# Decoder trunk on one core: elementwise sums move from GpSimd to VectorE, TensorE and adding transfers

## The chip, the core and the metric

The kernel runs on one NeuronCore of a Trainium2 chip. The engines are called as in the profile: PE (TensorE, matrix products), DVE (VectorE), ACT (ScalarE), POOL (GpSimd), SP (SyncE, which here only starts transfers). Transfers are started from a queue of an engine and carried out by 16 DMA engines. The metric is the time of one execution on the device in microseconds (us).

## The reference, cut to what matters

All numbers are fp32; T = 528 tokens (16 of them learned), D = 1024 channels. Two layers, each a mixer and a gated MLP:

```
h = h + fox_conformer_mixer(rms_norm(h))         # layer 0
   proj = x @ w_in                               # q, k, v, f (8 heads of 64), glu (2 x 512)
   a, g = split(glu);  u = a * sigmoid(g)
   u = causal_depthwise_conv(u, conv_w) + conv_b # width 31, 512 channels
   u = silu(layer_norm(u))
   out = concat(forgetting_attention(q, k, v, f), u) @ w_out
h = h + conv_glu_ffn(rms_norm(h))                # up to 2 x 2816, conv of width 3, silu(gate)*val, down
h = h + multiscale_pool_mixer(rms_norm(h))       # layer 1: windows 2, 4, 8, 16 over the tokens
   d_g = (cs - lag_w(cs)) / min(n, w) - x        # cs = cumsum over tokens, g = channel group
   y   = (d @ pool_w[g] + pool_b) * pool_scale
h = h + conv_glu_ffn(rms_norm(h))
out = rms_norm(h)[:, 16:]
```

## The kernel before, in words

Channels lie on the 128 partitions and tokens along them, so h is 8 tiles h0 to h7 of 128x528; what is 528 wide is multiplied in two halves of 264. PE works in the reduced fp32 format: every operand is split in a high part (a rounding copy) and a low part (the rest), and each product is three matmuls, wH with xH, wH with xL, wL with xH.

**Weights.** They come in 162 chunks of 8 tiles (512 KB), in the order in which PE wants them, through 3 buffers (4 in the second half). `prepare(c)` makes each chunk: SP's queue loads `raw`, ACT (or DVE for the 20 chunks in `VECTOR_CHUNKS`) copies it to `wH`, ACT writes `wL` = -wH, and POOL's queue starts a transfer that adds `raw` onto `wL` (L179, `accum_op=add`). This adding transfer is the only one of its size before the change.

**Stages of the trace.** Start and first norm to 34 us; the mixer of layer 0 to 286 us; its MLP ("up" and "dn" products) to 666 us; the pooling mixer, with the first up tiles of the second MLP inside it, to 722 us; the rest of that MLP and the output to the end.

**The mixer.** `PE_ORDER` sets PE's order by hand: pairs of a/g projections, then q, k, v by head pairs, with the attention's products between them. The convolution has 4 tiles of 31 taps each. Tap 0 is on ACT. A tap of kind 0 is one DVE instruction (L495: cv += u shifted, times its column of weights); one of kind 1 is a product on ACT into `tap` (2 buffers, L498) and an addition on POOL (L499). Tiles 0 and 2 and 28 taps of tile 3 are kind 0 (88 instructions), tile 1 and taps 1 and 2 of tile 3 kind 1 (32). `fill(pace)`, called at each F of `PE_ORDER`, hands out taps of both kinds by the table `PACE`. DVE also empties PE's sums (u L465, sg L472, q L561, k L579, v L598, o L738), splits the attention's weights (PL L718) and takes its row maxima (L660). `ln_sum` adds up the four convolved tiles for the layer norm (`mu`), on POOL.

**The pooling mixer.** PE's and DVE's orders are written out by `POOL_ORDER`: Z scales z (the normalised h) by the norm's R, S is the window sum (for windows over 2 a scan), T the ratio at the first 16 tokens, D makes the difference and adds it to h (L1037), X splits h in xH (ACT) and xL (DVE, L260) and multiplies it with four up tiles, Q squares h for the next norm (ACT) and adds the square to `acc` (POOL, L249).

## Time and profile before

| | us |
|---|---|
| median of 3 runs | 1096.94 (1095.26 to 1097.67) |
| the profiled execution | 1095.61 |
| its span in the profile | 1093.5 |
| PE busy | 1037.5 (95%) |
| DVE busy | 586.6 (54%) |
| ACT busy | 622.4 (57%) |
| POOL busy | 306.1 (28%) |

The span runs from the first instruction to the last; the profiled execution's own time has some 2 us around it. The shares of busy time are means over stages that differ: PE is full in both MLPs and has its idle time at the start, in the mixer to 165 us, and in the pooling mixer.

### The profile page before, as it was taken

The page shows a single profiled execution, that of the slowest core. Times are in us where ns is not written, and L with a number is a line of the kernel's source. Part 1 is how long each engine was busy: PE and PEld are TensorE (multiplying, and loading weights), DVE is VectorE, ACT ScalarE, POOL GpSimd, SP SyncE. Part 2 cuts the span into 40 slices and gives each one's busy share as a digit, 9 for nine tenths or more (in the row PEclk, how much of TensorE's full clock was granted, in tenths as well). Part 3 has the DMA queues.
Part 4 walks back from the last instruction along what each step waited for, and adds up shares of the span by engine and source line. Part 5 has one row for each costly group of instructions (what it writes and reads, how often), then busy time and mean ns, then how long its engine had stood idle before and what let it go on. Part 6 is the DMA issues. An engine that isn't in the chain of part 4 may idle for free.

```text
span 1093.5 us, 20138 instructions
## 1 busy us (share of the span) xinstructions
PE 1037.5 (95%) x8356; PEld 1023.8 (94%) x8356; DVE 586.6 (54%) x868; ACT 622.4 (57%) x872; POOL 306.1 (28%) x397
## 2 busy tenths in 40 slices
PE   7988789999999999999999998789999999999996
PEld 6978689999999999999999998789999999999995
DVE  5799999886318741024454225927853015545213
ACT  6647656786448753345556657346755335655642
POOL 7666552323311111111111134531111111111222
PEclk9998899999999999999999999899999999999998
DMA  6755333536987778777888777458778878878762
GB/s 215 187 142 132 83 74 99 157 79 159 220 199 170 178 171 186 184 174 178 187 181 178 184 174 174 111 120 192 176 174 193 191 164 192 184 176 198 170 135 77
DMA packets 51995, 178.18 MB, mean 163 GB/s; under 512 B 6208, under 2 KB 8256, under 8 KB 51904
## 3 DMA queue, kind: packets, MB, share of 16 engines
q0 software_dynamic: 23840, 84.98, 42.7%
q1 hardware_dynamic: 26720, 90.68, 25.9%
q8 instruction: 66, 1.08, 0.4%
q10 hardware_dynamic: 1344, 1.23, 0.3%
q14 instruction: 25, 0.20, 0.1%
HBM read 89.80 MB, written 2.10 MB: 84 GB/s over the span
## 4 chain that ended last, share of the span: by engine, by line
PE 78%; DVE 13%; ACT 3%; issue 2%; DMA 2%; POOL 1%; DVEq 0%; SPq 0%; POOLq 0%; ACTq 0%
PE up L198 44%; PE dn L198 23%; DVE h L495 5%; PE wo L198 3%; PE ps_v L198 1%; PE ps_a L198 1%; PE s L198 1%; PE o L198 1%; DVE xL L260 1%; DVE N L660 1%; DVE ws L1023 1%; DVE PL L718 1%; PE ps_k L198 1%; DMA raw<-wts 1%; DVE ws L1035 1%
## 5 line engine op out<-in xcount | busy, mean ns | idle before, releaser
L179 POOL DMA_DIRECT2D wL<-raw x162 | 138.1, 852 | 644.5 <-ACT wL L178 609.6
L198 PE MATMUL up<-xL,wH 128*128 128x264 f32 (+1 forms) x1408 | 288.0, 286 | 13.5 <-DVE xL L260 13.5
L198 PE MATMUL up<-xH,wH 128*128 128x264 f32 (+1 forms) x1408 | 287.1, 285 | 1.9 <-ACT xH L259 1.9
L198 PE MATMUL up<-xH,wL 128*128 128x264 f32 (+1 forms) x1408 | 287.3, 286 | 0.0
L224 ACT CAST wH<-raw 128x1024 fp32r<-128x1024 f32 x142 | 149.0, 1050 | 220.6 <-PE up L198 110.7
L198 PEld LDWEIGHTS up<-xL,wH 128*128 128x128 f32 x1408 | 220.3, 191 | 15.0 <-DVE xL L260 15.0
L198 PEld LDWEIGHTS up<-xH,wH 128*128 128x128 f32 x1408 | 220.5, 190 | 2.5 <-ACT xH L259 2.5
L198 PEld LDWEIGHTS up<-xH,wL 128*128 128x128 f32 x1408 | 219.8, 191 | 0.2 <-DMA wL<-raw 0.2
L178 ACT ACTIVATE wL<-wH 128x1024 fp32r<-128x1024 f32 x162 | 170.5, 1052 | 40.0 <-DVE wH L225 17.2
L923 DVE SCALAR_TENSOR_TENSOR t<-u,par,t 128x528 f32<-128x528 f32 (+1 forms) x176 | 131.0, 759 | 57.1 <-ACT t L920 54.1
L198 PE MATMUL dn<-gH,wH 128*128 128x264 f32 (+1 forms) x704 | 146.1, 284 | 0.0
L198 PE MATMUL dn<-gL,wH 128*128 128x264 f32 (+1 forms) x704 | 145.9, 283 | 0.0
L198 PE MATMUL dn<-gH,wL 128*128 128x264 f32 (+1 forms) x704 | 145.6, 283 | 0.0
L974 DVE TENSOR_TENSOR h<-dn,h 128x528 f32<-128x528 f32 (+1 forms) x30 | 21.0, 700 | 176.0 <-PE dn L198 176.0
L198 PEld LDWEIGHTS dn<-gL,wH 128*128 128x128 f32 x704 | 110.4, 189 | 0.1
L198 PEld LDWEIGHTS dn<-gH,wH 128*128 128x128 f32 x704 | 110.2, 189 | 0.1
L198 PEld LDWEIGHTS dn<-gH,wL 128*128 128x128 f32 x704 | 109.8, 188 | 0.0
L953 DVE TENSOR_TENSOR u<-up,R 128x528 f32<-128x528 f32 (+1 forms) x74 | 51.7, 701 | 104.7 <-PE up L198 104.6
L495 DVE SCALAR_TENSOR_TENSOR h<-u,par,h 128x528 f32<-128x528 f32 x88 | 86.8, 999 | 0.9
L920 ACT ACTIVATE t<-u,par 128x528 f32<-128x528 f32 (+1 forms) x88 | 70.9, 820 | 2.0 <-DVE u L960 2.0
L249 POOL TENSOR_TENSOR acc<-acc,sq 128x528 f32<-128x528 f32 (+1 forms) x30 | 45.3, 1508 | 34.6 <-ACT sq L247 34.3
L499 POOL TENSOR_TENSOR h<-h,tap 128x528 f32<-128x528 f32 x32 | 49.4, 1543 | 11.1 <-ACT tap L498 9.9
(248 smaller groups left out, 1573.9 us busy)
## 6 DMA issues: line engine op xcount, KB each, us to landing
raw<-wts SPq DMA_DIRECT2D x162, 512.0 KB, 4.3
wL<-raw POOLq DMA_DIRECT2D x162, 512.0 KB, 5.8
h<-hT SPq DMA_DIRECT2D x8, 264.0 KB, 6.0
hm<-hT SPq DMA_DIRECT2D x8, 264.0 KB, 7.0
outT<-y ACTq DMA_DIRECT2D x1, 512.0 KB, 3.1
outT<-y SPq DMA_DIRECT2D x1, 512.0 KB, 3.9
par<-par SPq DMA_DIRECT2D x1, 476.5 KB, 6.6
outT<-y ACTq DMA_DIRECT2D x1, 384.0 KB, 2.8
```

The costliest lines, as they stand in the source:

```text
L178: nc.scalar.mul(wL, wH.bitcast(F32), -1.0)
L179: nc.gpsimd.dma_start(wL, raw, accum_op=ALU.add)
L198: nc.tensor.matmul(out, lhsT, rhs, start=start, stop=stop)
L224: return nc.scalar.copy(out, src)
L249: state["sum"] = nc.gpsimd.tensor_tensor(acc[:, t0:t1], acc[:, t0:t1], sq[:, t0:t1], op=ALU.add)
L260: nc.vector.scalar_tensor_tensor(xL[m][:, t0:], h[m][:, t0:], col(gcol + m), xH[m][:, t0:].bitcast(F32), op0=ALU.mult, op1=ALU.subtract)
L495: nc.vector.scalar_tensor_tensor(cv[i], src, cw(i, j), cv[i], op0=ALU.mult, op1=ALU.add)
L499: nc.gpsimd.tensor_tensor(cv[i], cv[i], pr, op=ALU.add)
L920: nc.scalar.activation(t_, uu[:, off + 2:off + 2 + nt], AF.Identity, scale=col(c0 + 2), bias=col(c0 + 3))
L923: nc.vector.scalar_tensor_tensor(t_, uu[:, off + x:off + x + nt], col(c0 + x), t_, op0=ALU.mult, op1=ALU.add)
L953: nc.vector.tensor_tensor(v2(ud), ps[:, :, :nu], v2(R[:, tu:tu + 2 * nu]), op=ALU.mult)
L974: nc.vector.tensor_tensor(v2(h[m][:, td:]), ps[:, :, :nd], v2(h[m][:, td:]), op=ALU.add)
```

## The change

GpSimd's elementwise additions and products go elsewhere:

- **Convolution.** Tile 0 (`ADDED`) becomes kind 1 whole: 29 products on ACT (taps 2 to 30), each added by a transfer of 264 KB from POOL's queue, by turns to `cv[0]` and a second sum `cv2` (which tap 1 starts, on ACT). DVE adds `cv2` to `cv[0]` in `ln_sum`. Tiles 1, 2 and 3 are 90 taps on DVE.
- **First norm.** PE sums the 8 squares itself (16 matmuls with ones in the loop of the first products); the additions on POOL and the separate sums behind the loop go.
- **Other norms.** The additions of squares go to DVE; in the pooling mixer they are adding transfers, which follow one another on `acc`.
- **Pooling.** The order is new; all of Z is on DVE; h's additions for tiles 1 to 5 are adding transfers, those of 0, 6 and 7 on DVE.
- **Smaller.** u times sigmoid, mu, var and f on DVE; copies of masks, P4, q, k and v on ACT; all wH copies on ACT; wL of the first three chunks by a subtraction on DVE in place of ACT and a transfer; `PACE` is new.

```diff
-        copy("V" if c in VECTOR_CHUNKS else "A", wH, raw)
-        nc.scalar.mul(wL, wH.bitcast(F32), -1.0)
-        nc.gpsimd.dma_start(wL, raw, accum_op=ALU.add)
+        nc.scalar.copy(wH, raw)
+        if c < FIRST_CHUNKS:                      # 3
+            nc.vector.tensor_tensor(wL, raw, wH.bitcast(F32), op=ALU.subtract)
+        else:
+            nc.scalar.mul(wL, wH.bitcast(F32), -1.0)
+            nc.gpsimd.dma_start(wL, raw, accum_op=ALU.add)
...
-            state["sum"] = nc.gpsimd.tensor_tensor(acc[:, t0:t1], acc[:, t0:t1], sq[:, t0:t1], op=ALU.add)
+            if by_dma:
+                nc.gpsimd.dma_start(acc[:, t0:t1], sq[:, t0:t1], accum_op=ALU.add)
+            else:
+                nc.vector.tensor_tensor(acc[:, t0:t1], acc[:, t0:t1], sq[:, t0:t1], op=ALU.add)
...
-                    nc.gpsimd.tensor_tensor(uu, uu, t_, op=ALU.mult)
+                    nc.vector.tensor_tensor(uu, uu, t_, op=ALU.mult)
                     for j in range(CW):
-                        queue[i % 2 if i < 3 or j < TAPS3 else 0].append((i, j))
+                        queue[int(i == ADDED)].append((i, j))
...
             if j == 0:
                 nc.scalar.activation(cv[i], src, AF.Identity, scale=cw(i, j), bias=col(C_CB + i))
+            elif kind == 1 and j == 1:
+                nc.scalar.activation(cv2, src, AF.Copy, scale=cw(i, j))
             elif kind == 0:
                 nc.vector.scalar_tensor_tensor(cv[i], src, cw(i, j), cv[i], op0=ALU.mult, op1=ALU.add)
             else:
                 pr = wk.tile([P, T], F32, tag="tapp", name=f"tap{i}_{j}")
                 nc.scalar.activation(pr, src, AF.Copy, scale=cw(i, j))
-                nc.gpsimd.tensor_tensor(cv[i], cv[i], pr, op=ALU.add)
+                nc.gpsimd.dma_start((cv[i], cv2)[j % 2], pr, accum_op=ALU.add)
...
+            sums = [sp(f"ssq{x}")[:, :TH] for x in range(2)]
             for k in range(KT):
+                sq = first_square(k)
...
+                square_sums(sums, 0, [sq], k == 0, k == KT - 1)
...
+            nc.vector.tensor_tensor(cv[ADDED], cv[ADDED], cv2, op=ALU.add)
             a1, a2 = sum_of(cv[0], cv[1], "mu0"), sum_of(cv[2], cv[3], "mu1")
-            nc.gpsimd.tensor_tensor(a1, a1, a2, op=ALU.add)
+            nc.vector.tensor_tensor(a1, a1, a2, op=ALU.add)
...
-                eng = nc.gpsimd if m in POOL_Z else nc.vector
-                eng.tensor_tensor(z[m][:, 16:], z[m][:, 16:], R, op=ALU.mult)
+                nc.vector.tensor_tensor(z[m][:, 16:], z[m][:, 16:], R, op=ALU.mult)
...
-            eng = nc.gpsimd if m in POOL_RES else nc.vector
-            eng.tensor_tensor(h[m], h[m], s_, op=ALU.add)
+            if m in POOL_RES:                     # (1, 2, 3, 4, 5)
+                nc.gpsimd.dma_start(h[m], s_, accum_op=ALU.add)
+            else:
+                nc.vector.tensor_tensor(h[m], h[m], s_, op=ALU.add)
...
-PACE = ((0.75, 0.25), (3.75, 5.0), (2.5, 4.5), (5.25, 1.25), (4.0, 1.0), (3.25, 3.0))
+PACE = ((1.4, 0.6), (2.2, 0.8), (4.5, 1.2), (4.5, 1.2), (4.5, 1.2), (4.5, 1.2))
```

**POOL in the middle of the convolution.** Before, between the adding transfers of weight chunks 11 to 13 (h1 is the sum of tile 1):

```order
L179 DMA wL11_981<-raw11_978 128x1024
L499 TENSOR_TENSOR h1_65<-h1_65,tap1_12_1015 128x528
L499 TENSOR_TENSOR h1_65<-h1_65,tap1_13_1018 128x528
L499 TENSOR_TENSOR h1_65<-h1_65,tap1_14_1021 128x528
L179 DMA wL12_1087<-raw12_1084 128x1024
L499 TENSOR_TENSOR h1_65<-h1_65,tap1_15_1024 128x528
L499 TENSOR_TENSOR h1_65<-h1_65,tap1_16_1027 128x528
L499 TENSOR_TENSOR h1_65<-h1_65,tap1_17_1069 128x528
L179 DMA wL13_1211<-raw13_1208 128x1024
```

Now, between those of chunks 9 to 12 (h0 and cv2 are the two sums of tile 0):

```order
L180 DMA wL9_821<-raw9_818 128x1024
L510 DMA h0_64<-tap0_10_1076 128x528
L510 DMA cv2_162<-tap0_11_1107 128x528
L180 DMA wL10_890<-raw10_887 128x1024
L510 DMA h0_64<-tap0_12_1175 128x528
L510 DMA cv2_162<-tap0_13_1243 128x528
L180 DMA wL11_967<-raw11_964 128x1024
L510 DMA h0_64<-tap0_14_1290 128x528
L510 DMA cv2_162<-tap0_15_1506 128x528
L510 DMA h0_64<-tap0_16_1509 128x528
L180 DMA wL12_1044<-raw12_1041 128x1024
```

The additions became transfers at the same places of the queue, two or three between two weight chunks, and the last of the 29 stands ahead of chunk 15.

**DVE where the second key pair is emptied** (ps_k1_1), some two thirds into the taps. Before:

```order
L579 TENSOR_TENSOR h5_69<-ps_k1_1_1433,R_365 128x264
L495 SCALAR_TENSOR_TENSOR h2_66<-u2_239,par_88,h2_66 128x528 x3
L586 TENSOR_TENSOR k2_1_0_225<-h5_69,k1_1_0_224 64x528
L495 SCALAR_TENSOR_TENSOR h2_66<-u2_239,par_88,h2_66 128x528
L586 TENSOR_TENSOR k2_1_1_231<-h5_69,k1_1_1_230 64x528
L495 SCALAR_TENSOR_TENSOR h2_66<-u2_239,par_88,h2_66 128x528
L718 TENSOR_TENSOR PL0_1_0_1494<-P0_1_0_1492,PH0_1_0_1493 128x384
L598 TENSOR_TENSOR h6_70<-ps_v1_0_1547,R_365 128x264
L495 SCALAR_TENSOR_TENSOR h2_66<-u2_239,par_88,h2_66 128x528
L718 TENSOR_TENSOR PL0_1_1_1506<-P0_1_1_1504,PH0_1_1_1505 128x272
L738 TENSOR_TENSOR h7_71<-o0_0_256_1473,rec0_0_256_1487 64x272
```

Now, from the split of the attention's weights just behind it:

```order
L505 SCALAR_TENSOR_TENSOR h3_67<-u3_214,par_88,h3_67 128x528
L505 SCALAR_TENSOR_TENSOR h2_66<-u2_213,par_88,h2_66 128x528
L601 TENSOR_TENSOR k2_1_0_199<-h5_69,k1_1_0_198 64x528
L505 SCALAR_TENSOR_TENSOR h3_67<-u3_214,par_88,h3_67 128x528
L505 SCALAR_TENSOR_TENSOR h2_66<-u2_213,par_88,h2_66 128x528
L601 TENSOR_TENSOR k2_1_1_205<-h5_69,k1_1_1_204 64x528
L782 TENSOR_TENSOR h0_64<-h0_64,cv2_162 128x528
L505 SCALAR_TENSOR_TENSOR h3_67<-u3_214,par_88,h3_67 128x528
L733 TENSOR_TENSOR PL0_1_0_1422<-P0_1_0_1420,PH0_1_0_1421 128x384
L505 SCALAR_TENSOR_TENSOR h2_66<-u2_213,par_88,h2_66 128x528
L733 TENSOR_TENSOR PL0_1_1_1434<-P0_1_1_1432,PH0_1_1_1433 128x272
L753 TENSOR_TENSOR h7_71<-o0_0_256_1401,rec0_0_256_1415 64x272
```

The sum of cv2 and h0, which needs the last adding transfer, now stands in DVE's order, with 16 taps, v1 and work of the attention behind it on the way to the first ps_k2.

**DVE in the pooling mixer**, from the scaling of z2 on. Before:

```order
L1013 TENSOR_TENSOR z2_7713<-z2_7713,R_7752 128x528
L1013 TENSOR_TENSOR z3_7714<-z3_7714,R_7752 128x528
L260 SCALAR_TENSOR_TENSOR xL0_80<-h0_64,par_88,xH0_72 128x528
L1023 SCALAR_TENSOR_TENSOR ws3_7921<-z3_7714 128x528
L1023 SCALAR_TENSOR_TENSOR ws2_7923<-z2_7713 128x528
L1030 TENSOR_TENSOR ws2_7923<-ws2_7923,par_88 128x16
L1030 TENSOR_TENSOR ws3_7921<-ws3_7921,par_88 128x16
L1035 SCALAR_TENSOR_TENSOR ws2_7923<-z2_7713,ws2_7923 128x528
L260 SCALAR_TENSOR_TENSOR xL1_81<-h1_65,par_88,xH1_73 128x528
L1035 SCALAR_TENSOR_TENSOR ws3_7921<-z3_7714,ws3_7921 128x528
L1013 TENSOR_TENSOR z5_7716<-z5_7716,R_7752 128x528
L1023 SCALAR_TENSOR_TENSOR ws4_7961<-z4_7715 128x528
```

Now:

```order
L1029 TENSOR_TENSOR z2_7706<-z2_7706,R_7745 128x528
L1039 SCALAR_TENSOR_TENSOR ws2_7914<-z2_7706 128x528
L1046 TENSOR_TENSOR ws2_7914<-ws2_7914,par_88 128x16
L1051 SCALAR_TENSOR_TENSOR ws2_7914<-z2_7706,ws2_7914 128x528
L1029 TENSOR_TENSOR z3_7707<-z3_7707,R_7745 128x528
L1039 SCALAR_TENSOR_TENSOR ws3_7920<-z3_7707 128x528
L264 SCALAR_TENSOR_TENSOR xL1_81<-h1_65,par_88,xH1_73 128x528
L1046 TENSOR_TENSOR ws3_7920<-ws3_7920,par_88 128x16
L1051 SCALAR_TENSOR_TENSOR ws3_7920<-z3_7707,ws3_7920 128x528
L1029 TENSOR_TENSOR z4_7708<-z4_7708,R_7745 128x528
L1039 SCALAR_TENSOR_TENSOR ws4_7953<-z4_7708 128x528
L264 SCALAR_TENSOR_TENSOR xL2_82<-h2_66,par_88,xH2_74 128x528
```

The order is a regular round of scale, scan, split of an earlier tile, ratio and difference, and no tile waits for a scaling on another engine.

**POOL there.** Before, from the addition of the first difference:

```order
L1037 TENSOR_TENSOR h1_65<-h1_65,ws1_7883 128x528
L1013 TENSOR_TENSOR z6_7717<-z6_7717,R_7752 128x528
L1037 TENSOR_TENSOR h2_66<-h2_66,ws2_7923 128x528
L179 DMA wL99_7893<-raw99_7890 128x1024
L1037 TENSOR_TENSOR h3_67<-h3_67,ws3_7921 128x528
L249 TENSOR_TENSOR acc_91<-acc_91,sq2_8067 128x528
L1037 TENSOR_TENSOR h4_68<-h4_68,ws4_7961 128x528
L179 DMA wL100_7970<-raw100_7967 128x1024
L1037 TENSOR_TENSOR h5_69<-h5_69,ws5_7963 128x528
```

Now, from the same difference:

```order
L1053 DMA h1_65<-ws1_7909 128x528
L180 DMA wL99_7881<-raw99_7878 128x1024
L1053 DMA h2_66<-ws2_7914 128x528
L251 DMA acc_91<-sq1_7955 128x528
L1053 DMA h3_67<-ws3_7920 128x528
L251 DMA acc_91<-sq2_7997 128x528
L1053 DMA h4_68<-ws4_7953 128x528
L251 DMA acc_91<-sq3_8032 128x528
L1053 DMA h5_69<-ws5_7995 128x528
L180 DMA wL100_7963<-raw100_7960 128x1024
```

Additions of h and of squares became transfers in one queue with those of the weights; an h addition stands behind the square of two tiles before.

## Rows read from the trace of the kernel before

**Rows 1.** The page's busy time by engine.

```profile
PE 1037.5 (95%) x8356; PEld 1023.8 (94%) x8356; DVE 586.6 (54%) x868; ACT 622.4 (57%) x872; POOL 306.1 (28%) x397
```

**Rows 2.** Stretches: length, busy time by engine (instructions), granted clock, DMA share, GB/s.

```profile
43.70:165.00 121.30, 101.17 (x743) 96.97 (x743) 118.26 (x165) 69.73 (x118) 75.00 (x68) 0.90 0.48 114
165.00:200.00 35.00, 34.60 (x293) 33.38 (x293) 33.19 (x69) 23.92 (x54) 10.99 (x15) 1.00 0.39 92
165.00:286.30 121.30, 118.75 (x972) 114.60 (x971) 95.34 (x194) 81.68 (x162) 37.88 (x50) 1.00 0.53 132
330.00:600.00 270.00, 270.00 (x2214) 270.00 (x2213) 125.23 (x174) 152.26 (x177) 43.27 (x84) 1.00 0.79 180
666.00:722.20 56.20, 41.87 (x293) 39.85 (x292) 45.88 (x46) 28.38 (x44) 31.84 (x32) 0.91 0.53 125
```

**Rows 3.** Waits of PE, 43.7 to 165 us: total, times, longest.

```profile
PE o L198 <- DVE PL L718: 4.4, 2, 3.0
PE e L198 <- DVE E L664: 4.1, 2, 2.4
...
PE ps_g L198 <- DVE u L465: 3.2, 2, 2.3
```

**Rows 4.** DVE's taps (L495) in two stretches: length, busy (count), clock, DMA share, GB/s.

```profile
43.70:165.00 121.30, 70.65 (x67) 0.90 0.48 114
165.00:200.00 35.00, 16.18 (x21) 1.00 0.39 92
```

**Rows 5.** DVE's line of time: start, length, instruction; the first tap, the first ps_k2.

```profile
43.72 0.76 DVE L495 SCALAR_TENSOR_TENSOR h<-u,par,h 128x528 f32<-128x528 f32 x1
...
165.05 0.43 DVE L579 TENSOR_TENSOR h<-ps_k,R 128x264 f32<-128x264 f32 x1
```

**Rows 6.** PE's line of time from the first products to the second.

```profile
21.20 2.11 PE L198 MATMUL ps_a<-xH,wL 128*128 128x264 f32 x16
...
25.92 0.48 PE L198 MATMUL ps_g<-xH,wH 128*128 128x264 f32 x1
```

**Rows 7.** DMA of 38 to 118 us: packets, MB, share of 16 engines; issues, us to landing.

```profile
q0 software_dynamic: 1696, 5.26, 35.8%
q1 hardware_dynamic: 1645, 5.95, 21.9%
...
wL<-raw POOLq DMA_DIRECT2D x10, 512.0 KB, 4.6
```

**Rows 8.** The same issues at 330 to 600 us.

```profile
wL<-raw POOLq DMA_DIRECT2D x47, 512.0 KB, 6.1
```

**Rows 9.** Their issue on POOL from 50 to 280 us, ns min/median/max.

```profile
L179 POOL DMA_DIRECT2D wL<-raw x24: 846/864/914, 51.1 to 276.5; - x24
```

**Rows 10.** Plain transfers of 2.1 KB from POOL's queue (L590).

```profile
DMA to landing us min/median/max: 1.8/4.5/6.5
```

**Rows 11.** The product of a tap on ACT.

```profile
L498 ACT ACTIVATE tap<-u,par x32: 718/732/777, 54.7 to 147.3; 128x528 f32<-128x528 f32 x32
```

**Rows 12.** PE's waits, 666 to 724 us.

```profile
PE up L198 <- DVE xL L260: 12.4, 6, 3.9
```

**Rows 13.** DVE's line of time in the pooling mixer: its first and last work.

```profile
675.44 0.71 DVE L1013 TENSOR_TENSOR z<-z,R 128x528 f32<-128x528 f32 x1
...
717.06 2.40 DVE L260 SCALAR_TENSOR_TENSOR xL<-h,par,xH 128x528 fp32r<-128x528 f32 x1 [1.80 <-ACT xH L259]
```

**Rows 14.** DVE's lines of the pooling mixer: ns min/median/max, first and last start.

```profile
L1013 DVE TENSOR_TENSOR z<-z,R x5: 694/697/1806, 675.4 to 699.6; 128x528 f32<-128x528 f32 x5
...
L1023 DVE TENSOR_TENSOR_SCAN ws<-z x6: 1226/1764/2381, 684.3 to 705.9; 128x528 f32<-128x528 f32 x6
...
L1030 DVE TENSOR_TENSOR ws<-ws,par x6: 161/170/176, 686.7 to 707.3; 128x16 f32<-128x16 f32 x6
...
L1035 DVE SCALAR_TENSOR_TENSOR ws<-z,ws x6: 702/1264/2171, 686.9 to 710.9; 128x528 f32<-128x528 f32 x6
...
L260 DVE SCALAR_TENSOR_TENSOR xL<-h,par,xH x30: 734/1353/2403, 5.1 to 717.1; 128x528 fp32r<-128x528 f32 x30
```

More of the change, by code (lines that the diff above doesn't have):

```diff
@@ L237, in use_log_exp, with squares @@
         return ld
-    def squares(m, apart, t0=0, t1=T, part=True):
+    def squares(m, apart, t0=0, t1=T, part=True, by_dma=False):
         if m == 0:
@@ L335, in trunk_kernel, with first_square @@
         state["emitted"] = 3
-        for m in range(KT):
-            i_ = squares(m, APART[0], part=SPLIT_FIRST)
+        def first_square(m):
+            sq = wk.tile([P, T], F32, tag="sq", name=f"sq{m}", bufs=3)
+            i_ = nc.scalar.activation(sq, h[m], AF.Square)
             if SQ_AFTER[m] is not None:
                 after(i_, xs_[SQ_AFTER[m]])
+            return sq
         ident = pt[:, C_ID:C_ID + P]
@@ L351, in trunk_kernel @@
         cv = h[0:4]
+        cv2 = mp.tile([P, T], F32, tag="cv2", name="cv2")
         scr = h[4:8]
@@ L388, in late @@
         def late(ap, x):
-            after(nc.gpsimd.memset(ap, x), state["sum"])
+            nc.gpsimd.memset(ap, x)
         def constants():
@@ L413, in constants @@
                 for c0 in (0, P + NMETA):
-                    after(nc.gpsimd.tensor_copy(to[:, c0:c0 + P], tri), state["sum"])
+                    nc.scalar.copy(to[:, c0:c0 + P], tri)
         H8 = slice(0, HEADS)
@@ L528, in first_products @@
                 nc.scalar.copy(low[:, half(hf)], ps[32:40, :])
-            nc.gpsimd.tensor_tensor(cell["f"], cell["f"], low, op=ALU.add)
+            nc.vector.tensor_tensor(cell["f"], cell["f"], low, op=ALU.add)
+            return sums
         def gate_sums():
@@ L756, in sum_of @@
         def sum_of(x, y, name):
-            t_ = wk.tile([P, T], F32, tag="sq", name=name)
-            nc.gpsimd.tensor_tensor(t_, x, y, op=ALU.add)
+            t_ = wk.tile([P, T], F32, tag="sq", name=name, bufs=3)
+            nc.vector.tensor_tensor(t_, x, y, op=ALU.add)
             return t_
@@ L786, in ln_mean @@
                 else:
-                    nc.gpsimd.tensor_tensor(cell["var"], cell["var"], s_, op=ALU.add)
+                    nc.vector.tensor_tensor(cell["var"], cell["var"], s_, op=ALU.add)
         def ln_var():
-            rs = wk.tile([P, T], F32, tag="sq", name="rstd")
+            rs = wk.tile([P, T], F32, tag="sq", name="rstd", bufs=3)
             rsqrt(rs, channel_mean(cell["var"], "var"), 1.0 / (P * NCONV), eps[:, 1:2])
@@ L837, in trunk_kernel @@
                 if n_ == NORM_AT:
-                    cell["R"] = inv_rms([sp(f"ssq{x}")[:, :TH] for x in range(2)], 0)
+                    cell["R"] = wk.tile([P, T], F32, tag="R", name="R", bufs=1)
+                    rsqrt(cell["R"], sums, 1.0 / D, eps[:, 0:1])
                     for fn, hf, ps in pending:
@@ L1049, in trunk_kernel @@
             begun, step = up_side(1, [(j, s) for j in range(OUTER[1] // 2) for s in range(2)])
-            stages = {"Z": scale_z, "S": window, "T": ratio, "D": residual, "X": follow, "Q": lambda m: squares(m, APART[3])}
+            stages = {"Z": scale_z, "S": window, "T": ratio, "D": residual, "X": follow, "Q": lambda m: squares(m, APART[3], by_dma=True)}
             for name in POOL_ORDER.split():
```

26 lines of the change are left out of this document (12 added, 14 removed).

## The prediction

> **What bounds the kernel now.** I read the page's busy time first: PE works 95% of the span [rows 1]. A change that takes nothing off PE can then win only in the stretches where PE is not full, so next come the stretches [rows 2]. At 330 to 600 us PE is busy all the time, and from 165 to 286 us for 118.75 of 121.3 us; it falls behind in two places. From 43.7 to 165 us it works 101.2 of 121.3 us at a mean granted clock of 0.90, while DVE works 118.3. In the pooling mixer (666 to 722.2 us) it works 41.9 of 56.2. Third, who keeps it waiting: in the first of these the largest waits all end with DVE [rows 3], in the second 12.4 us end with DVE's xL [rows 12]. So DVE's list of work sets both stretches, and whatever time leaves one of them goes off the whole: what follows is full PE.
>
> Fourth, why DVE takes so long. A tap takes 70.65/67 = 1.054 us from 43.7 to 165, and 16.18/21 = 0.770 from 165 to 200 [rows 4]. The other instructions take (118.26 - 70.65)/98 = 0.486 in the first stretch and (33.19 - 16.18)/48 = 0.354 in the second [rows 2, 4]. POOL is busy 62% of the first stretch, all its tap additions among it, and 31% of the second, where most of that is issue of transfers. At the second stretch's prices the first one's 67 taps and 98 others are 86 us; DVE loses 32 us beside POOL.
>
> **DVE's work in the mixer, after.** In the printed order DVE has, from its first tap to the emptying of the first ps_k2, 90 taps and 97 others. At 0.770 and 0.354 that is 69.3 + 34.3 = 103.6 us, against 121.3 from 43.7 to 165.05 [rows 5]: 23 more taps, and still 18 us less. I take the low prices, since POOL has next to no elementwise work left in this stretch; at the high ones it would be 142 us. The first tap now belongs to tile 1 instead of tile 0, one pair of projections later, but PE starts earlier: it no longer sums squares between 23.3 us, where the first products end, and 25.9 [rows 6], and the first three wL come from DVE. I put the first tap at 45 us (43 to 48). With 2 us of waits the end would be 150.6, 14 us earlier.
>
> **The adding transfers.** No row shows one of 264 KB. From below, 2.1 KB from the same queue landed in 1.8 us at the least [rows 10]; from above, 512 KB in a median of 4.6 [rows 7], and of 6.1 where the DMA share was 0.79 [rows 2, 8]. By size between 1.8 and 4.6, 264 KB is some 3.2 us with the DMA engines as they were.
>
> They won't be as they were. From 38 to 118 us the two large queues took 35.8 and 21.9% of the engines, 46.2 us for 10 chunks, of which 28.6 were the wL transfers [rows 7]. So a chunk costs 4.6 us of all engines, its adding transfer 2.86, and one of 264 KB 1.48; 29 make 43 us. In POOL's printed order the last stands ahead of chunk 15, so wL3 to wL14 and about 14 loads go before it: 12 x 2.86 + 14 x 1.75 = 59 us, 102 with the taps. Some 13 us of this fit in before 38 us, where the first can start; the other 89 end at 127 us with the engines full, at 132 with them 95% full. I take 128. The same by round trips: two `tap` buffers allow two in flight, each takes its landing, 0.73 us of ACT [rows 11] and some 0.5 us of queueing; 29 (L + 1.2) / 2 from 38 us ends at 128 for a landing L of 5 us, which I take; at 3.2 it ends at 102.
>
> DVE stands at the sum of cv2 and h0 after 74 taps and 54 others, 57.0 + 19.1 = 76.1 us, so with 2 us of waits at 123. It waits 5 us there, with v1, work of the attention and 16 taps queued behind it up to that ps_k2, and PE waits for those. The remaining 16 taps and 43 others are 27.5 us, and with 2 us of waits the first ps_k2 is emptied at 157.5: **7.5 us won in the mixer**.
>
> In POOL's queue an adding transfer also waits for the one before it on the same sum, with wL transfers behind it. Chunks are wanted every 121.3/12 = 10 us on average here, so a wL some us late has cover; where PE takes one each 48 x 270/2214 = 5.9 us [rows 2], as at the start, it has not, and the lead at the start is what pays.
>
> **The pooling mixer.** DVE's work there at the shortest durations [rows 14]: 8 scalings 5.6, 2 window sums at the price of a scaling 1.4, 6 scans 7.4, 6 ratios 1.0, 6 differences 4.2, 3 additions to h 2.1, 8 xL 5.9: 27.6 us. From R at 675.4 [rows 13] the last xL would end at 703, against 719.5 now. What can wait is in the printed round: between the difference of tile m and the xL of m stand one difference, two scalings, two scans and one xL, about 5.3 us, in which the transfer must land and ACT write xH. Two rounds are 7.0 us of DVE work; the loop through the transfer is L + 3 (xH, xL, ratio, difference and issue), so below 4 us it costs nothing, at 5 us it costs 0.5 a round, 2.5 over five. The squares' additions share the queue: one must land before the next, and the h addition of two tiles later stands behind it. The engines get 12 x 1.48 = 18 us on top of the 0.53 x 56.2 = 30 of before, in a shorter stretch, so 5 us is my value here too. With 1 us for the queue xL ends at 706.5; before, X7's products end 2.7 us behind the last xL, at 722.2 where the stretch ends; then at 709.2, 13 us sooner; **I take 12**. The last square lands some 6 us after X7; its sum is wanted three up tiles of 48 products later, 17 us, so that is covered.
>
> **The rest** I count at nothing: squares of the other norms on DVE lie under full PE (DVE is busy 125 of 270 us in the MLP [rows 2]), the 20 copies wH under ACT's 152 of 270; in the mixer ACT has 70 of 121 busy, and some ten copies and ten smaller ones leave it below 90.
>
> Sum: 7.5 + 12 = 19.5 off the profiled 1095.6, so 1076. The median of the runs is 1.3 above the profiled time: **1077 us**.
>
> **A rule against the row.** POOL's wL issues took 846 to 914 ns with DVE busy 97% of the time [rows 2, 9], and landed in 4.6 us. The Trainium skill (SBUF — State Buffer, section "SBUF: two separate sides") warns that GpSimd can't write a transfer's descriptors while DVE holds their shared port. The narrow spread does not show it here; by that rule a landing would be longer by up to one tap, an estimated 0.77 us, and the time some 13 us higher, the third case below. The Trainium skill (DMA: Bandwidth & Descriptors, section "Anatomy of one DMA — SWDGE (gpsimd) path") gives 2.0 us plus bytes over 436e3 for such a transfer; by it 264 KB is an estimated 2.6 us and 512 KB 3.2. The row has 4.6 for 512 KB, so the row decides; by the page nothing would wait for cv2, which is the second case below.
>
> **The rivals.**
> - *The transfers keep up* (landing up to 4.2 us): the DMA share of 0.48 [rows 2] speaks for it, the 43 us of transfers put before chunk 15 against. No wait for cv2: 14 us in the mixer, 15 in pooling, 1067 to 1068.
> - *Late transfers make it slower.* The place is the sum of cv2: taps end at 55.4 + 14.5 L, the stretch 29.5 us later. Against 165 that is 14.5 L - 80; pooling gives 2.5 L - 25. Together nothing is left at L = 6.2 us; at 7 us it is 14 slower, 1111. For it: 512 KB took 6.1 us where the share was 0.79 [rows 8], and here it comes near 1. Against: half the bytes, and only two in flight.
> - *In between* (5.4 to 6 us): 3 to 13 us won, about 1088.
> - *DVE is not freed*, because transfers slow it as additions did: 90 taps at 1.054 end the stretch near 178, pooling wins little, 1108. Against it: 21 taps at 0.770 in a stretch with DMA at 0.39 [rows 2, 4].
> - *PE's start counts for more*: with the first tap at 43 and no waits anywhere 18 and 17 us are won, 1062.
>
> **Chances.** The forecast (14 to 25 us won) 0.42; transfers keep up 0.20, with the larger lead 0.06; in between 0.14; late transfers 0.13; not freed 0.03; within 0.2%, which is about what a measurement of this kernel can tell from no change, 0.02. So faster 0.82, same 0.02, slower 0.16. The range is 1057 to 1098: down to that last case with 5 us more of lead at the start, which no row excludes, and up to a landing of 6.2 us.
>
> **What would show it.** Taps of 0.77 us on DVE throughout; 264 KB landing in 5 us from 40 to 130 us with the DMA share over 0.85; DVE idle some 5 us before the sum with cv2, released by a transfer; the first ps_k2 emptied near 158; X7 ending 33 us after R instead of 47; nothing between 165 and 666 us or after 722 changed in length. I am wrong if taps stay above 0.9, or if landings are well off 5 us: each 1 us of landing moves the sum by 17.

## The result and the profile after

The changed kernel takes 1082.21 us (median of 4 runs, 1081.33 to 1083.29) against 1097.31 for the kernel before on the same chip: a ratio of 0.9862, 95% interval 0.9839 to 0.9885. That is 15.1 us off; 20 had been forecast, 1077 in a range of 1057 to 1098. The profiled execution took 1082.84, its span 1081.0, so of the two profiled executions the changed one is 12.8 us the faster.

The time came out near the forecast. Of the two terms of its sum, the pooling mixer's held in the main and the mixer's did not. These are the stretches that answer to [rows 2], of the changed kernel (length, busy time of PE, PE's weight loads, DVE, ACT, POOL with the number of instructions, granted clock, DMA share, GB/s):

```profile
43.70:165.00 121.30, 95.01 (x711) 90.57 (x711) 97.78 (x184) 73.06 (x121) 42.28 (x55) 0.90 0.82 173
165.00:200.00 35.00, 34.60 (x294) 33.39 (x293) 21.67 (x53) 23.98 (x55) 4.89 (x9) 1.00 0.36 86
165.00:286.30 121.30, 119.50 (x988) 116.34 (x988) 80.51 (x187) 90.00 (x180) 14.58 (x26) 1.00 0.54 135
666.00:722.20 56.20, 50.52 (x384) 48.33 (x384) 31.41 (x48) 34.62 (x52) 16.13 (x28) 0.97 0.84 179
```

In the pooling mixer PE works 8.7 us more of the same stretch than before. In the mixer it works 6.2 us less, at the same clock, although DVE now has 23 us of the stretch free and POOL is down from 75 to 42: the engine that was full is no longer full, and the stretch is no shorter for it. The DMA share is up from 0.48 to 0.82.

DVE's taps, the counterpart of [rows 4] (the first stretch now holds all 90):

```profile
43.70:165.00 121.30, 65.60 (x90) 0.90 0.82 173
```

That is 0.729 us each. But the first ps_k2 is emptied at 168.6, not at 157.5 and not even at the 165.05 of [rows 5]; DVE's line of time:

```profile
49.34 2.38 DVE L505 SCALAR_TENSOR_TENSOR h<-u,par,h 128x528 f32<-128x528 f32 x3 [0.62 <-ACT h L501]
...
141.67 0.71 DVE L782 TENSOR_TENSOR h<-h,cv 128x528 f32<-128x528 f32 x1
...
168.56 0.43 DVE L594 TENSOR_TENSOR h<-ps_k,R 128x264 f32<-128x264 f32 x1
```

The sum with cv2 starts at 141.7 (DVE had been expected there at 123, for a wait of 5 us), and DVE does not wait at it. It has waited earlier, and for ACT. Waits of DVE and then of ACT, from 43.7 to 165 and from 40 to 150 us (total, times, longest):

```profile
DVE PL L733 <- ACT P L732: 8.4, 2, 7.8
DVE u L487 <- ACT sg L481: 6.5, 2, 3.5
DVE h L505 <- ACT h L501: 3.1, 2, 2.5
DVE k L601 <- ACT k L225: 2.9, 2, 2.1
```

```profile
ACT tap L508 <- DMA h<-tap: 17.2, 9, 3.6
ACT tap L508 <- DMA cv<-tap: 16.1, 10, 3.8
```

Read together: 33 us of ACT go by with a tap's product at the head of its queue, waiting for one of the two `tap` buffers, which a transfer that has not landed still reads. Behind it stand the sigmoids, the attention's exponentials and the copies of q and k that DVE and PE want. PE's counterpart to [rows 3] names them:

```profile
PE e L199 <- DVE E L679: 7.0, 3, 3.3
PE s L199 <- ACT q L691: 4.8, 2, 4.1
PE tv L627 <- ACT P L732: 4.3, 1, 4.3
...
PE ps_a L199 <- DMA wL<-raw: 2.3, 1, 2.3
```

For weights, whose transfers stand in the same queue, PE waits 2.3 us: they are not what holds it.

The chain of work from 43.7 to 150 us, by line, says it in one row (it is cut at its end by the view): 59% of it are the two kinds of adding transfers.

```profile
by line: DMA cv<-tap 37.7%; DMA h<-tap 21.6%; issue 12.0%; DMA wL<-raw 5.9%; PE ps_k L199 4.0%; DVE h L505 3.6%; ACT tap L508 2.9%; DVE PL L733 1.6%; PE o L199 1.2%; ACT wH L174 1.0%; ACT wL L179 0.9%; POOL k L606 0.8%; POOL h L510 0.8%; PO
```

The transfers themselves (their issue on POOL, first and last start; their time to landing; then the counterpart of [rows 7] for 38 to 118 us):

```profile
L510 POOL DMA_DIRECT2D h<-tap x15: 853/862/1125, 42.3 to 137.6; - x15
...
DMA to landing us min/median/max: 3.3/4.9/9.7
```

```profile
q0 software_dynamic: 4704, 10.85, 76.0%
q1 hardware_dynamic: 1445, 5.26, 19.2%
...
wL<-raw POOLq DMA_DIRECT2D x10, 512.0 KB, 6.7
h<-tap POOLq DMA_DIRECT2D x11, 264.0 KB, 5.2
cv<-tap POOLq DMA_DIRECT2D x11, 264.0 KB, 5.2
```

The two queues hold the engines for 95% of the time, and 264 KB land in 5 us, as forecast. Both groups together are the 29 transfers of which 28 intervals lie between 42.3 and 137.6: 3.4 us each, where 3.1 had been taken, from a start at 42 instead of 38. The first queue's 76.0% of 80 us, less 28.6 for its 10 wL as in [rows 7], leaves 32.2 us of the engines for 22 transfers of 264 KB, an estimated 1.46 each; 1.48 had been priced.

The pooling mixer, the counterparts of [rows 14] (ns min/median/max, first and last start) and of [rows 12]:

```profile
L1029 DVE TENSOR_TENSOR z<-z,R x8: 698/701/707, 674.6 to 700.5; 128x528 f32<-128x528 f32 x8
...
L1039 DVE TENSOR_TENSOR_SCAN ws<-z x6: 1257/1258/1259, 681.0 to 701.2; 128x528 f32<-128x528 f32 x6
...
L1051 DVE SCALAR_TENSOR_TENSOR ws<-z,ws x6: 707/707/708, 682.5 to 703.3; 128x528 f32<-128x528 f32 x6
```

```profile
PE up L199 <- ACT xH L263: 3.5, 2, 2.6
PE up L199 <- DVE xL L264: 2.2, 6, 0.7
```

These durations are within 3% of the shortest of before and hardly spread, and PE's 12.4 us of waits for xL are 2.2, with 3.5 for xH.

A table of stages, in us, from the lines of time (first product of g, of the output projection, of the first MLP, R of the pooling mixer, the next R, the span), shows where the 12.5 us of the span lie:

| | before | changed |
|---|---|---|
| g begins | 25.9 | 26.6 |
| output projection begins | 218.1 | 218.5 |
| first MLP begins | 278.0 | 279.4 |
| R of the pooling mixer (its last half begins) | 675.0 | 674.2 |
| R of the second MLP | 745.7 | 734.5 |
| end | 1093.5 | 1081.0 |

The mixer lost 1.4 us; the first MLP, with its norm's additions off POOL, won 2.2; the pooling mixer won 10.4 (70.8 to 60.4 from R to R), the rest 1.3.

Each column is one execution, and the kernels below repeat its stages with the same code, so they show how far such numbers carry. Runs 6 and 9 have the changed kernel's mixer and begin the first MLP at 278.7 and 278.1; run 5 has the mixer of before and begins it at 278.5. So the new mixer won nothing and lost at most about 1 us. Runs 1 to 5 and 8 have the changed pooling mixer, and it takes 60.5 to 63.3 us in them (66.5 in run 7): 10.4 us is the most that it won in any of these traces.

The change has two parts more, which its list does not name: a third buffer for the squares and sigmoids (`sq`), and `dynamic_dma_scratch_size=8192` for the program. No run tries either alone.

### The profile page after: what moved, and what is told of

Its sections match the earlier page's. It is cut to its first block, busy times and chain, and to the rows that moved or that the text cites. A ratio compares the mean times of both kernels' runs of the same rounds, so it can differ in the third digit from the quotient of the medians.

```text
span 1081.0 us, 20159 instructions
## 1 busy us (share of the span) xinstructions
PE 1033.4 (96%) x8376; PEld 1019.9 (94%) x8376; DVE 532.2 (49%) x888; ACT 643.3 (60%) x906; POOL 208.3 (19%) x331
## 4 chain that ended last, share of the span: by engine, by line
PE 81%; DMA 8%; DVE 5%; issue 3%; ACT 3%; POOL 0%; DVEq 0%; SPq 0%; POOLq 0%; ACTq 0%
PE up L199 46%; PE dn L199 23%; DMA cv<-tap 4%; PE wo L199 3%; DMA h<-tap 2%; PE ps_k L199 1%; PE ps_v L199 1%; PE o L199 1%; PE pl L199 1%; PE m L199 1%; PE ps_q L199 1%; DVE h L505 1%; PE s L199 1%; PE ssq L199 1%; DMA h<-ws 1%
## 5 line engine op out<-in xcount | busy, mean ns | idle before, releaser
L174 ACT CAST wH<-raw 128x1024 fp32r<-128x1024 f32 x162 | 169.8, 1048 | 228.4 <-PE up L199 115.3
L179 ACT ACTIVATE wL<-wH 128x1024 fp32r<-128x1024 f32 x159 | 167.3, 1052 | 1.8
L505 DVE SCALAR_TENSOR_TENSOR h<-u,par,h 128x528 f32<-128x528 f32 x90 | 65.6, 761 | 3.6 <-ACT h L501 3.1
L216 ACT CAST gH<-t 128x528 fp32r<-128x528 f32 (+1 forms) x44 | 27.5, 624 | 43.8 <-DVE t L951 43.6
L217 DVE TENSOR_TENSOR gL<-t,gH 128x528 fp32r<-128x528 f32 (+1 forms) x44 | 30.8, 700 | 25.7 <-ACT gH L216 25.6
```

The source lines that it names most:

```text
L174: nc.scalar.copy(wH, raw)
L179: nc.scalar.mul(wL, wH.bitcast(F32), -1.0)
L216: nc.scalar.copy(oH, src)
L217: nc.vector.tensor_tensor(oL, src, oH.bitcast(F32), op=ALU.subtract)
L505: nc.vector.scalar_tensor_tensor(cv[i], src, cw(i, j), cv[i], op0=ALU.mult, op1=ALU.add)
```

## The experiments

Two theories were open after the result. The first: the mixer is now held by the mass of adding transfers, through ACT's queue. The second: it is held by something else, ACT's added copies or PE's order, and the transfers are only busy beside it. Ratios below are to the kernel before, in the same session, with 95% intervals.

**1. Without the transfers.** Tile 0's taps 2 to 30 are left out.

```diff
-                        queue[int(i == ADDED)].append((i, j))
+                        if i != ADDED or j < 2:
+                            queue[int(i == ADDED)].append((i, j))
```

> The changed kernel without taps 2 to 30 of tile 0: neither their products on ACT nor their 29 adding transfers are there, so that part of the convolution is left out. Theory A (in the mixer the 29 transfers set the pace: a product waits on ACT for a buffer that frees only when a transfer lands after some 5 us, and ACT's work for the attention waits behind it): DVE runs its 103.6 us from a first tap at 49 with few waits, the first ps_k2 is emptied near 155 instead of 168.6, time 1068 to 1071. Theory B (the mixer is held by something else, ACT's added copies and the later first tap): less than 3 us won, 1079 to 1083.

Measured: 1058.88 us, ratio 0.9659 (0.9636 to 0.9682). The first tap begins at 44.2 instead of 49.3, the first ps_k2 is emptied at 143.5 instead of 168.6:

```profile
143.49 0.43 DVE L595 TENSOR_TENSOR h<-ps_k,R 128x264 f32<-128x264 f32 x1
```

From the first tap DVE needs 99.3 us for its list, so 103.6 was a fair price for it. What lies between 143.5 and 168.6 is the transfers and their products. The second theory is out; the first had under-estimated them: 23 us against the 11 to 14 expected. This run takes away the products and the transfers together and does not tell them apart; run 4 does.

**2. More buffers.** The products get 4 buffers instead of 2 (`bufs=4`).

> The changed kernel with 4 buffers for the products of the taps instead of 2. The two sums still take one transfer each at a time. If it is ACT's queue, held by products that wait for a buffer, that costs (theory A1): ACT runs ahead by two products and lets the attention's work pass, 3 to 8 us won, 1074 to 1079. If it is the rate of the transfers (theory A2): the last still lands near 138 to 142 us, and DVE, which now has the sum with cv2 after 60 taps instead of 74, waits there: 1081 to 1086.

Measured: 1089.38, ratio 0.9937 (0.9914 to 0.9959): slower than the changed kernel, and outside the ranges of both theories. ACT is held a little less (29 us for taps) and the last transfer starts at 121.9 instead of 137.6, 3.0 us apart. But the sum with cv2 comes after 60 taps, and now DVE does wait there:

```profile
DVE h L782 <- DMA h<-tap: 11.6, 1, 11.6
```

It goes on at 126.5, close to the 128 of the forecast, with 30 taps and not 16 still to do, and empties the first ps_k2 at 171.2. The DMA share from 38 to 118 us is 1.00 here. With ACT less in the way, the rate of the transfers is the limit that is left, and the wait moves to the place that the prediction named. The longer queue did not help with the DMA engines full.

**3. Fewer transfers.** Taps 2 to 10 of tile 0 go to DVE into h0, the other 19 into two sums of their own (tap 11 starts cv3). Taps 2 and 3 run ahead of the start of h0 here and are overwritten, so these two are missing from the sum.

```diff
-                        queue[int(i == ADDED)].append((i, j))
+                        queue[int(i == ADDED and not 2 <= j < 11)].append((i, j))
...
-                nc.gpsimd.dma_start((cv[i], cv2)[j % 2], pr, accum_op=ALU.add)
+                nc.gpsimd.dma_start((cv2, cv3)[j % 2], pr, accum_op=ALU.add)
```

> Nine taps of tile 0 (2 to 10) on DVE into h0, the other 19 as transfers into two sums of their own, cv2 and cv3 (tap 11 starts cv3 on ACT), and two sums on DVE. Theory A: the transfers end 10 x 3.3 = 33 us sooner, DVE works 9 x 0.77 + 0.7 = 7.6 us more in time in which it waits now; first ps_k2 near 160, time 1073 to 1077. Theory B: DVE's list is longer by 7.6 us and nothing else moves, 1083 to 1090.

Measured: 1077.64, ratio 0.9837 (0.9808 to 0.9865). The first ps_k2 comes at 160.7, as the first theory expected. The interval overlaps the changed kernel's, so the time alone does not decide; the line of time does (the output projection begins 7.9 us sooner, and 5.9 to 7.0 sooner than in runs 6 and 9, which have the changed kernel's mixer).

**4. The additions back on GpSimd.** The same 29 additions, on the same two sums, as instructions:

```diff
-                nc.gpsimd.dma_start((cv[i], cv2)[j % 2], pr, accum_op=ALU.add)
+                to = (cv[i], cv2)[j % 2]
+                nc.gpsimd.tensor_tensor(to, to, pr, op=ALU.add)
```

> The changed kernel with the 29 additions of tile 0 as GpSimd instructions on the same two sums by turns instead of adding transfers; all else as changed. Theory A (DVE loses to GpSimd's additions what it loses beside them in the kernel before, and transfers cost it nothing): taps of DVE above 0.95 us while the 29 additions run (some 45 us of GpSimd), about 17 us more DVE work, but ACT held no more; first ps_k2 at 165 to 172, 1079 to 1086. Rival (additions on GpSimd were the cheaper way, and what the mixer loses now is the transfers): 1070 to 1077.

Measured: 1094.10, ratio 0.9985 (0.9971 to 1.0000): the pooling mixer's gain is in it (60.9 us from R to R), and the mixer loses as much (the first MLP begins at 289.0). The direction is theory A's; the loss is larger than its 1079 to 1086, and the first ps_k2 comes at 178.9. DVE's taps up to 150 us, first in this kernel, then in the changed one:

```profile
43.70:150.00 106.30, 81.24 (x74) 0.84 0.41 100
```

```profile
43.70:150.00 106.30, 57.94 (x80) 0.89 0.89 185
```

1.098 us a tap beside GpSimd's additions, 0.724 beside the adding transfers at a DMA share of 0.89. The mean hides two kinds of taps. These are the durations of single ones (ns min/median/max) before, in this kernel and in the changed one:

```profile
L495 DVE SCALAR_TENSOR_TENSOR h<-u,par,h x88: 746/764/2419, 43.7 to 197.7; 128x528 f32<-128x528 f32 x88
...
L505 DVE SCALAR_TENSOR_TENSOR h<-u,par,h x90: 746/762/6411, 48.0 to 175.8; 128x528 f32<-128x528 f32 x90
...
L505 DVE SCALAR_TENSOR_TENSOR h<-u,par,h x90: 746/761/771, 49.3 to 164.0; 128x528 f32<-128x528 f32 x90
```

The medians are equal. Of the taps up to 150 us 22 of 60 took over 1 us before and 20 of 74 in this kernel; in the changed one none did. So the ground of the forecast, that DVE loses to GpSimd's additions and not to transfers, is shown directly. As a way of adding 29 products the transfers are some 12 us cheaper than GpSimd, and still dearer than they need be (run 7).

The run also parts ACT's products from the transfers. The products and their two buffers are as in the changed kernel, but ACT waits 8.4 us for a buffer from 40 to 150 us, and not 33, and the last addition starts at 121.4 and not at 137.6:

```profile
ACT tap L508 <- POOL cv L511: 4.5, 5, 1.4
ACT tap L508 <- POOL h L511: 3.9, 4, 1.4
```

**5. The pooling mixer's change alone**, put into the kernel before: its order, Z on DVE, the transfers for h and the squares, the addition to h7 on DVE, wH of chunks 96 to 107 on ACT, and the two parts that the list does not name.

```diff
-                eng = nc.gpsimd if m in POOL_Z else nc.vector
-                eng.tensor_tensor(z[m][:, 16:], z[m][:, 16:], R, op=ALU.mult)
+                nc.vector.tensor_tensor(z[m][:, 16:], z[m][:, 16:], R, op=ALU.mult)
...
-            eng = nc.gpsimd if m in POOL_RES else nc.vector
-            eng.tensor_tensor(h[m], h[m], s_, op=ALU.add)
+            if m in POOL_RES:
+                nc.gpsimd.dma_start(h[m], s_, accum_op=ALU.add)
+            else:
+                nc.vector.tensor_tensor(h[m], h[m], s_, op=ALU.add)
```

> The kernel before with the change of the pooling mixer alone (its order, all of Z on DVE, h's and the squares' additions as adding transfers, the wH copies of chunks 96 to 107 on ACT). Theory: the pooling mixer gave 10 to 12 us of the 15 and the mixer about nothing, so 1084 to 1087, with the mixer's end at 278 us as before. Rival: the mixer's part gave more than its line of time shows (its lead is spent later): above 1090.

Measured: 1084.33, ratio 0.9905 (0.9889 to 0.9920), 10.3 us; R to R 60.8 us, the first MLP beginning at 278.5. The rival is out: this part alone is most of the gain.

**6. GpSimd's additions in the pooling mixer.** Order and Z as changed, the 5 additions of h and the 7 of squares as GpSimd instructions instead of transfers.

> The changed kernel with GpSimd instructions for the additions of h (tiles 1 to 5) and of the squares in the pooling mixer in place of adding transfers; its new order and Z on DVE stay. Theory (DVE loses beside GpSimd's additions): DVE's scans and differences lengthen there again, xL late, 5 to 8 us of the pooling mixer's gain gone, 1087 to 1090. Rival (the gain is from the order and Z on DVE, and a transfer of 4 us is no quicker than an addition of 1.7): 1079 to 1083.

Measured: 1089.08, ratio 0.9953 (0.9937 to 0.9969). R to R is 69.6 us again, and DVE's scans and its ratios of 16 columns, beside 1.26 us and 0.17 in the changed kernel, are

```profile
L1039 DVE TENSOR_TENSOR_SCAN ws<-z x6: 1259/2254/2272, 680.2 to 708.2; 128x528 f32<-128x528 f32 x6
...
L1046 DVE TENSOR_TENSOR ws<-ws,par x6: 161/728/1791, 682.6 to 710.0; 128x16 f32<-128x16 f32 x6
```

So the new order is not what wins; taking GpSimd's additions away is. The stretch from R to R, in the changed kernel and in this one (columns as in [rows 2]):

```profile
674.15:734.53 60.38, 54.70 (x423) 52.64 (x422) 29.82 (x47) 36.38 (x53) 18.22 (x21) 0.97 0.87 186
...
673.40:742.95 69.55, 57.95 (x423) 56.35 (x422) 41.91 (x46) 36.48 (x53) 28.57 (x21) 0.90 0.55 131
```

Of the 9.2 us 5.9 are PE's idle time (11.6 us in place of 5.7). The other 3.3 are longer busy time for as many matmuls: the mean granted clock is 0.90 in place of 0.97, that is, PE is longer at the lower level of its clock (0.50, 1.2 GHz) and shorter at the upper one (1.00, 2.4 GHz). In the kernel before it is 0.93 there.

**7. All taps on DVE.** No product, no transfer in the convolution.

```diff
-                        queue[int(i == ADDED)].append((i, j))
+                        queue[0].append((i, j))
...
-PACE = ((1.4, 0.6), (2.2, 0.8), (4.5, 1.2), (4.5, 1.2), (4.5, 1.2), (4.5, 1.2))
+PACE = ((2.0, 0), (3.0, 0), (5.7, 0), (5.7, 0), (5.7, 0), (5.7, 0))
```

> The changed kernel with all taps of the convolution on DVE, no product on ACT and no adding transfer there. By the run without tile 0's taps (first ps_k2 at 143.5) plus 29 taps at 0.73: first ps_k2 near 165, PE fed later only by that, 1079 to 1082 if DVE's list alone sets the mixer. Theory that the transfers are worth their place: slower than the changed kernel, above 1084. Theory that they cost more than they take off DVE: below 1080.

Measured: 1074.64, ratio 0.9817 (0.9801 to 0.9834): faster than the changed kernel, by 7.6 us or, by the ratios, 5. The first ps_k2 is emptied at 154.1, better than the 165 expected, since DVE starts on tile 0 at 38.2 and so has work where it stood idle. The chain from 43.7 to 150 us is DVE's again:

```profile
by line: DVE h L505 60.7%; DVE N L675 6.8%; PE ps_k L199 4.8%; PE ps_q L199 4.3%; DVE PL L733 3.1%; DVE h L576 2.1%; DVE k L601 2.0%; DVE u L487 1.7%; PE e L199 1.7%; DVE h L753 1.5%; DVE h L613 1.4%; DVE q L584 1.3%; DVE sg L480 1.3%; DVE 
```

Of the 14 us by which the first MLP begins sooner than in the changed kernel (12.5 sooner than in run 9), 6.1 are lost in the pooling mixer (R to R 66.5): h's transfers take 6.3 us to land in the median there, up to 8.0, with those of weights in the same queue, and PE waits 8.1 us for xH in place of 3.5. PE's idle time is 4.1 of the 6.1; the other 2.1 are longer busy time, at a mean granted clock of 0.92 in place of 0.97.

**8. Rounded squares.** The first norm's squares in PE's reduced format, which also rounds them.

```diff
-            sq = wk.tile([P, T], F32, tag="sq", name=f"sq{m}", bufs=3)
+            sq = wk.tile([P, T], F32R, tag="sq", name=f"sq{m}", bufs=3)
```

> The changed kernel with the first norm's squares rounded to PE's reduced fp32 format, so that each of the 16 matmuls with ones is one pass and not two. The 8 pairs took 1.05 us each in a loop in which PE was full from 11 us on; now 0.4. Theory (PE's sums in the loop cost the lead at the start that was forecast): second products begin at 21 to 23 us instead of 26.6, first tap 3 to 4 us sooner, 1077 to 1080. Rival (DVE's and ACT's work sets the loop, or the transfers take the lead back): 1081 to 1083.

Measured: 1085.32, ratio 0.9915 (0.9894 to 0.9936). The mechanism is there: g begins at 20.4 instead of 26.6, the first tap at 43.5. But the 26.6 is late. The nine other traces with plain squares on PE (runs 1 to 4, 6, 7, 9, 10, 12) begin g at 22.8 to 25.0, so rounding moves g by some 2 to 5 us in this run (and by 1 to 3 in run 11, where g begins at 21.9). PE from 11 to 15 us, in the changed kernel and in run 6, which has the same start (columns as in [rows 2]):

```profile
11.00:15.00 4.00, 4.00 (x16) 3.27 (x16) 3.99 (x8) 1.74 (x3) 3.71 (x11) 0.57 0.95 385
...
11.00:15.00 4.00, 4.00 (x29) 3.55 (x27) 3.94 (x7) 3.42 (x10) 3.71 (x11) 1.00 0.89 364
```

PE is busy all the time in both and does about half the matmuls in the first, mostly at the lower level of its clock (0.50, 1.2 GHz). Before that it had waited 0.6 and 1.1 us for DVE's xH and xL; run 8 has waits of 1.3 and 1.1 at the same places and keeps the upper level, so why the clock fell stays open.

The gain is not there: the DMA share from 38 to 118 us is 0.99, the output projection begins 3 us sooner (1 to 2 us sooner than in runs 6 and 9), and the pooling mixer takes 63.3 us instead of 60.4. Its spread of runs (1082.85 to 1087.47) leaves open whether it is slower or the same.

**9 to 11. The additions of h in the pooling mixer on DVE** (`POOL_RES = ()`): in the changed kernel, with all taps on DVE, and that with rounded squares.

> The changed kernel with the additions of h in the pooling mixer all on DVE (tiles 1 to 5 too, 5 x 0.71 = 3.5 us more), the squares still as transfers. Theory (the five transfers' landings of 4 to 8 us, in one queue with weights, cost the loop more than the additions take off DVE): no wait of DVE on xH over 1 us, from R to the next norm's R some 57 to 59 us instead of 60.4, 1079 to 1081. Rival (they pay): DVE's longer list sets the end, 62 to 64 us, 1084 to 1086.

> All taps and all of h's additions on DVE. With all taps on DVE the stretch from R to the next norm's R took 66.5 us, since an addition of h stood behind a transfer of weights and landed after 8 us. Theory: that stretch comes to 57 to 60 us, 7 us off, 1066 to 1069. Rival (the stretch is longer there for another reason, PE's clock or the weights): 1073 to 1075.

> As the run before, with the first norm's squares rounded to PE's reduced format. With transfers in the convolution this put the mixer's end 2.8 us forward and the pooling mixer lost it again. Theory (the lead is real once no transfer eats it): 2 to 4 us below the run before, 1063 to 1066. Rival (DVE's list in the mixer begins no sooner): the same within 1 us.

Measured: 1083.30 (0.9886, 0.9864 to 0.9909), 1072.81 (0.9795, 0.9768 to 0.9821) and 1077.19 (0.9828, 0.9801 to 0.9856). R to R is 63.1, 64.0 and 69.1 us. The ninth is between theory and rival, and no faster: from R to R DVE waits 1.5 us for xH in place of 4.1, but has the 3.5 us more. The tenth is the fastest of the versions that do all the work, but the 2.5 us that it wins in the pooling mixer over the seventh are less than the 7 expected, and its interval overlaps the seventh's. Its time is close to the rival's 1073 to 1075. The granted clock is 0.97 there, so it is not the clock: PE waits 7.5 us for xL, with DVE's longer list, and 2.7 for ACT's copies. The eleventh fails its theory, and shows what is late next; ACT's line of time there:

```profile
693.08 0.74 ACT L263 ACTIVATE xH<-h,par 128x528 fp32r<-128x528 f32 x1 [2.87 <-DVE h L1054]
704.87 0.63 ACT L216 CAST acc_rv<-acc 128x528 fp32r<-128x528 f32 x1 [8.49 <-DMA acc<-sq]
705.41 1.56 ACT L966 COPY u<-up 128x516 f32<-128x516 f32 x3
```

The split of the squares' sum stands in ACT's queue ahead of the copies that free PE's accumulators, and waits 8.5 us for the seventh transfer of a chain in which each waits for the one before. PE then waits 5.8 us for those copies. This is 2.4 us more idle time of PE than in the tenth; another 2.7 us of the 5.1 are longer busy time at a lower mean clock (0.90, in the tenth 0.97):

```profile
661.72:730.82 69.10, 56.53 (x422) 55.01 (x422) 33.14 (x51) 36.27 (x53) 13.71 (x16) 0.90 0.71 160
```

In the changed kernel the copies stand ahead of the split, at 709.8 and 719.6.

**12. A few transfers.** The tenth, with tile 0's taps 22 to 30 as a second sum: one start on ACT, eight transfers one after the other; `PACE` is set between those of the changed kernel and of run 7.

> All of h's additions on DVE; tile 0's taps 22 to 30 as a second sum, started on ACT with tap 22, eight adding transfers onto it one after the other, and one sum on DVE; the other taps on DVE. Theory (a few transfers land in DMA time that is free, and only their mass hurts): DVE has 9 x 0.73 - 0.7 = 6 us less to do before the first ps_k2, 4 to 6 us below the run with all taps on DVE, 1061 to 1064. Rival (any adding transfer costs ACT and the weights as much as it saves): no faster than that run, 1066 to 1070.

Measured: 1074.24, ratio 0.9803 (0.9777 to 0.9829), no faster than the tenth. They land in a median of 4.0 us, the sum is there at 82.5 without a wait; but DVE waits 5.4 us for sigmoids on ACT, which now stand behind products (1.4 in the tenth), and 1.2 for the start of a tile's sum, and the first ps_k2 comes at 155.6 instead of 154.1. The rival holds in its order, though not in its time (both ranges were counted from the time that the tenth was expected to take): even eight cost ACT as much as they save DVE.

## Why the prediction was right in its time, and where it was not

- **What bounds the kernel** held: PE was full behind both stretches, and what a stretch won or lost went off the whole (1.4 us of the mixer apart, which the first MLP's own 2.2 covered).
- **DVE's loss to GpSimd** held. Priced from 165 to 200 us at 0.770 a tap; it is 0.729 in the changed kernel and 1.098 with the additions back (run 4), and the list took 99.3 us in run 1, priced at 103.6. Behind the sum with cv2 it took 26.9 us in the changed kernel, priced at 27.5.
- **The landing** of 5 us held (4.9 in the median, 5.2 at the densest), with the DMA share over 0.85 that was given as its sign. The end of the transfers at 128 held where ACT did not hold them (126.5 in run 2); in the changed kernel it was 141. Of these 13 us 4.3 are the later start; nearly all the rest is 14 round trips of 6.8 us in place of 6.2.
- **The step that failed** is the round trip's "0.73 us of ACT and some 0.5 us of queueing", with the statement that its copies "leave it below 90" of 121 us and so cost nothing. No row showed the 0.5 us; with a mean landing of 5.0 us the round trip of 6.8 leaves 1.8 for what was priced at 1.2. The larger miss is what the sum leaves out. ACT was busy for 73 us, below 90 as priced, and blocked for 33 more: a product that waits for a buffer holds up what stands behind it in ACT's queue, and the attention needs that. So in place of a wait of 5 us at the sum DVE had 20.9 us of waits for ACT before it, on P, sg, k and the starts of the sums. The mixer's 7.5 us won were 1.4 lost in the profiled execution (between nothing and 1.4 with runs 6 and 9). That ACT is where the wait sits is shown by the waits, and that the transfers and not the products are its cause by run 4, where ACT waits 8.4 us for the same buffers; run 1 gives what both cost together, and run 2 shows that the buffers alone are no cure.
- **The lead at the start** was not there in the profiled execution: PE was to start g earlier than before and DVE the taps at 45 (43 to 48), but g began 0.7 us later and the taps at 49.3. The sums in the loop had been given no price; unrounded, they took 0.88 us a pair, with PE full from 11 us on, and in this execution the clock was low besides (run 8). The nine other traces with these sums begin g 1 to 3 us sooner than before. Little comes of such a lead while the transfers set the pace: g begins 3.1 us sooner in run 6 than in the changed kernel, and the output projection 0.9.
- **The pooling mixer's 12 us** were 10.4, by the mechanism that was given (runs 5 and 6): 8.7 less idle time of PE, and 1.7 less busy time, with the clock at 0.97 in place of 0.93, which had no term. The other traces with the same code won 7.4 to 10.2 (4.2 in run 7); the last xL ended at 706.3, forecast 706.5. The cover for the chain of squares (wanted three up tiles later) held in this order of ACT's queue and failed in another (run 11).
- **The rest at nothing** was 3.5 us of gain. The first MLP's 2.2 go with its norm's additions off POOL: run 5, which keeps them there, has 0.3 of it; whether they are the cause was not tried. The 1.3 at the end do not: run 5 has them too (346.4 us from R to the end, before 347.8), with the additions of the last norm still on POOL.
- That the time is within 5 us of the forecast is in part luck. In the profiled executions the mixer gave 8.9 us less than forecast, pooling 1.6 less, and 3.5 came that had been counted at nothing: 12.5 of 19.5. The medians of the runs are 15.1 apart. The time lies at the edge between the forecast's case (14 to 25 us won) and the one in between (3 to 13). What held the mixer, ACT's queue, was in none of the rivals.

The Trainium skill's rule on descriptors (SBUF — State Buffer, section "SBUF: two separate sides") did not show: the 29 issues on POOL took 862 ns in the median (853 to 1279), as the 24 of before (864), beside taps at 0.73 us. The section names DVE operations in a 2-port mode for it, and no run here shows whether a tap is one. Its figures for such a transfer (DMA: Bandwidth & Descriptors, section "Anatomy of one DMA — SWDGE (gpsimd) path") give an estimated 2.6 us for 264 KB; the least landing here was 3.3, so the measurement decides.

The fastest version is the tenth, with all taps and h's additions on DVE and only the squares of the pooling mixer as transfers: 1072.81 us, with the seventh's 1074.64 within its interval. Open is what the pooling mixer would take in it with the split of the squares' sum behind the copies; this was not tried.
